# Half of a projection tile placed between the split of the first norm's sums and their products with ones

## The chip, the cores and the metric

The kernel runs on one core of one Trainium2 chip. The metric is the device time of one execution in microseconds (us). Its engines are called here as the profile calls them: PE (TensorE, matrix products), PEld (its weight loads), DVE (VectorE), ACT (ScalarE), POOL (GpSimd) and SP (SyncE, which issues nearly all DMAs). Each engine works through its own instructions in a fixed order, and waits for the others by semaphores.

## The reference

One layer (`DEPTH = 1`) on a sequence of 1024 tokens with 1024 channels, in float32. What the change touches is the very start: the first RMSNorm and the wide projection behind it.

```python
def rmsnorm(x, gain):
    xf = x.astype(jnp.float32)
    y = xf * lax.rsqrt(jnp.mean(xf * xf, axis=-1, keepdims=True) + EPS)
    return (y * gain.astype(jnp.float32)).astype(x.dtype)

def hybrid_layer(x, ...):
    h = rmsnorm(x, g_mix)
    proj = h @ w_in            # 8208 columns: attention q,k,v | forget logits | short conv |
                               # DeltaNet q,k,v, beta, decay, out gate | 3 branch gates
    ...                        # forgetting attention, gated short conv, gated DeltaNet
    x = x + merged @ w_o
    ...                        # channel mixer with a causal conv, then a per-layer embedding
    return x
```

## The kernel before

Activations lie transposed: 128 channels on the partitions, 1024 tokens along the free axis, in two halves of 512 (`NB[0]`, `NB[1]`; `nb` counts them). Eight such tiles `xg` hold the normed input's channels, without the norm's factor: `xg` is x times the gain, and the factor per token, `rs`, is multiplied in when a projection is copied out of PSUM. Since a matrix product takes operands of reduced precision (`fp32r`), each float32 operand is split into a high part (an ACT copy) and a low part (a DVE or POOL subtraction, x - high), and each product is three matmuls: high by high, high by low, low by high. A 128x128x512 block so costs three matmuls, and one output half of a projection tile (8 blocks, `KT = 8`) 24.

A **raw tile** is a projection of 128 output channels that is written to HBM as it is, without `rs`, for later use. `raw_tile(u)` loads and splits its weight (`wr`, then `wo` for the two halves of its rows) and returns a function `evac(nb, ps)` that copies a finished half from PSUM with ACT (`o<-sm` or `o<-mm`, line 504) and stores it to `raw[u]` by an SP DMA (line 505).

`first_norm()` runs in this order of code:

- It loads x tile by tile, makes `xg` (lines 270 and 271), adds up the squares over the eight tiles in `acc[0]` and `acc[1]` (lines 278 and 280), and meanwhile multiplies the few logits (`few`), the first query tile (`pq`) and one raw tile (`pr_`).
- `make_rstd(acc)` forms `rs`. For each half it splits the sums into `h` (ACT, line 289) and `l` (DVE, line 290), multiplies both with a 128x128 matrix of ones (two matmuls into one PSUM bank), and takes the inverse square root with three ACT operations (lines 257 to 259) and two DVE operations (lines 260 and 264). `between` is a hook that another norm uses: work that is put between the splits and the products. Here it is not given.
- A second raw tile is multiplied, half 0 and then half 1, each into a bank of the role `sm`.

The buffers count: `h` and `l` have one buffer each (`h=1, l=1` in the phase `fx`), the split weights `wo` five (`WO = 5`), and the role `sm` five PSUM banks in this phase, two in the next one; the roles `mm` and `ev` have two and one.

After it come, in the code, the logits (`few_logits`: the `sm` tile times `rs`, eight small transposes at line 396, and two DVE copies at lines 399 and 400), the query and key tiles, `scalars()` (a chain of some fifty small DVE operations on the logits that ends in `gall`, line 456; PE transposes `gall` at line 458, and it goes to HBM as `cdr` and comes back as `cb` for the attention), the value tile (copied out with a multiplication by `rs` at line 543, transposed by PE into the bank `ev` at line 546, copied out of it at lines 549 and 550), and the attention with projection tiles between its blocks.

The order on each engine isn't that of the code. A scheduler with a timeline of its own (`schedule_with_timeline_sim=True`) places each instruction when it is built, so a local edit can reorder a stretch behind it. Instructions that are given `tc.issue_after(x)` are placed behind x.

Of the kernel before, what the change touches and what calls it, by code (L numbers as in the profile page):

```python
# [48 lines left out]
def hybrid_block(ctx: ExitStack, tc: tile.TileContext, I, out, dbg=None):  # L49
# [5 lines left out]
    def nm(s):  # L55
        uid[0] += 1
        return f"{s}_{uid[0]}"
# [25 lines left out]
    def pt(tag, bufs, w=512, dt=F32):  # L83
        pool, n = homes.setdefault(tag, (scopes[-1], bufs))
        return pool.tile([P, w], dt, tag=tag, name=nm(tag), bufs=n)

    def bank(role):
        pool, n = homes[role]
        return pool.tile([P, 512], F32, tag=role, name=nm(role), bufs=n)
# [4 lines left out]
    def smb():  # L94
        return bank("sm")
# [4 lines left out]
    def tmp(role="tmp", dt=F32, w=512):  # L100
        return pt(role if role in homes else "tmp", 0, 516, dt)[:, 0:w]
# [21 lines left out]
    pe = [None]  # L123

    def mm(o, l, r, start, stop, more=False):
        pe[0] = nc.tensor.matmul(o, lhsT=l, rhs=r, start=start, stop=stop, skip_group_check=more)  # L126
# [20 lines left out]
    def wload(src, n=1024, eng=None):  # L147
        wr = wraw(src, n)
        return [wsplit(wr[:, c : min(c + 512, n)], eng or weng[0]) for c in range(0, n, 512)]

    def step(ps, w, j, x, nb, first, last):
        h, l = x
        wh, wl = w[j // 4]
        sl = slice(j % 4 * P, j % 4 * P + P)
        mm(ps, wh[:, sl], h[:, NB[nb]], first, False)
        mm(ps, wh[:, sl], l[:, NB[nb]], False, False)
        mm(ps, wl[:, sl], h[:, NB[nb]], False, last)
# [93 lines left out]
    def rsqrt(ps, scale, neg=False, t=None):  # L251

        w = ps.shape[-1]
        y = tmp("y") if w == 512 else small(w)
        if t is None:
            t = tmp("t") if w == 512 else small(w)
        S.activation(t, ps, AF.Ln, scale=scale)
        S.activation(y, t, AF.Exp, scale=-0.5)
        S.activation(t, y, AF.Square)
        V.scalar_tensor_tensor(out=t, in0=t, scalar=(0.5 if neg else -0.5) * scale, in1=ps, op0=ALU.mult, op1=ALU.mult)  # L260
        return t, y

    def newton(o, t, y, neg=False):
        V.scalar_tensor_tensor(out=o, in0=t, scalar=-1.5 if neg else 1.5, in1=y, op0=ALU.add, op1=ALU.mult)

    def norm_operand(kt, x, c):

        h, l = (xp.tile([P, T], F32R, tag="xg", name=nm("xg")) for _ in range(2))
        for nb in range(2):
            S.activation(h[:, NB[nb]], x[:, NB[nb]], AF.Copy, scale=col(c + kt))  # L270
            V.scalar_tensor_tensor(out=l[:, NB[nb]], in0=x[:, NB[nb]], scalar=col(c + kt),
                                   in1=h.bitcast(F32)[:, NB[nb]], op0=ALU.mult, op1=ALU.subtract)
        return h, l

    def sumsq(acc, x, first, eng=(G, G)):
        for nb in range(2):
            sq = acc[nb] if first else tmp("sq")
            last = S.activation(sq, x[:, NB[nb]], AF.Square).ins  # L278
            if not first:
                eng[nb].tensor_tensor(out=acc[nb], in0=acc[nb], in1=sq, op=ALU.add)  # L280
        return last

    def make_rstd(acc, between=None):

        r = cp.tile([P, T], F32, tag="rs", name=nm("rs"))
        parts = []
        for nb in range(2):
            h, l = tmp("h", F32R), tmp("l", F32R)
            S.activation(h, acc[nb], AF.Copy)
            V.scalar_tensor_tensor(out=l, in0=acc[nb], scalar=D * EPS / P, in1=h.bitcast(F32),  # L290
                                   op0=ALU.add, op1=ALU.subtract)
            parts.append((h, l))
        after = between() if between else None
        for nb in range(2):
            h, l = parts[nb]
            ps = smb()
            with tc.issue_after(after) if after else nullcontext():
                mm(ps, ones_r, h, True, False)
                mm(ps, ones_r, l, False, True)
            newton(r[:, NB[nb]], *rsqrt(ps, 1.0 / D))  # L300
        return r
# [22 lines left out]
    def first_norm():  # L324
        ones_f = pt("ones_f", 1, P)
        V.memset(ones_f, 1.0)
        V.tensor_copy(ones_r, ones_f)
        wsr, wsp = pt("wsr", 1, P), pt("wsp", 1, 256, F32R)
        pair = wsp.rearrange("p (k t c) -> p k t c", t=2, c=16)
        S.dma_start(wsr, I["wsm"])  # L330
        S.activation(pair[:, :, 0], wsr.rearrange("p (k c) -> p k c", c=16), AF.Copy)
        V.tensor_tensor(out=pair[:, :, 1], in0=wsr.rearrange("p (k c) -> p k c", c=16),
                        in1=pair[:, :, 0].bitcast(F32), op=ALU.subtract)
        acc = [pt("acc", 2) for _ in range(2)]
        xr = [pt("xr", 8, T) for _ in range(KT)]
        few, pq, pr_ = ([bank(r) for _ in range(2)] for r in ("sm", "mm", "sm"))
        for kt in range(KT):
            for nb in NB if kt == 0 else (slice(0, T),):
                Q.dma_start(xr[kt][:, nb], I["xT"][kt][:, nb])
            xg.append(norm_operand(kt, xr[kt], C_G1))  # L340
            if kt == 0:
                wq = wload(I["win"][U_FQ], eng=V)
            if kt == 2:
                wr, _, _, evac = raw_tile(spare["r"].pop(0), V)
            if kt:
                sumsq(acc, xr[kt - 1], kt == 1, (V, V))
        sumsq(acc, xr[KT - 1], False, (V, V))
        for kt in range(KT):
            for nb in range(2):
                h, l = xg[kt]  # L350
                for n, x in ((32, h), (16, l)) if kt == 0 else ((16, l), (32, h)):
                    mm(few[nb][:n], wsp[:, kt * 32 : kt * 32 + n], x[:, NB[nb]], kt == 0 and n == 32,
                       kt == KT - 1 and n == 32)
            for w, ps in ((wq, pq), (wr, pr_)):
                for nb in range(2):
                    step(ps[nb], w, kt, xg[kt], nb, kt == 0, kt == KT - 1)
        for nb in range(2):
            evac(nb, pr_[nb])
        Q.dma_start(cst, I["cst"])
        Q.dma_start(rows, I["rows"])  # L360
        V.tensor_copy(bd_r, bdf)
        V.tensor_copy(U_r, Uf)
        early[U_FQ] = pq
        rs = make_rstd(acc)
        w, _, _, evac = raw_tile(spare["r"].pop(0))
        for nb in range(2):
            ps = bank("sm")
            for kt in range(KT):
                step(ps, w, kt, xg[kt], nb, kt == 0, kt == KT - 1)
            evac(nb, ps)  # L370
        return rs, few

    def exp32(x):
# [124 lines left out]
    def raw_tile(u, eng=None):  # L498

        raw[u] = dr.tile([P, T], F32, tag=f"r{u}", name=f"r{u}")  # L500

        def f(nb, ps):
            o = tmp("o")
            S.activation(o, ps, AF.Copy)  # L504
            Q.dma_start(raw[u][:, NB[nb]], o)
        return wload(I["win"][u], eng=eng), KT, xg, f
# [383 lines left out]
    with phase("fx", psum=dict(mm=MM, ev=1), cv=3, o=4, sg=2, h=1, l=1, y=1,  # L890
               smt=1, Y=1, ye=1, en=1, er=1, Yz=1, Yq=1, lfh=1, lfl=1):
        with phase("f0", psum=dict(sm=5), tmp=8):
            rs, few = first_norm()
            smt = few_logits(few)
# [64 lines left out]
    with phase("la", psum=dict(mm=6, sm=2), a=16, wq=3):  # L959
        with phase("me", tmp=9, sg=4, yr=4):  # L960
# [83 lines left out]
            acc = [tmp() for _ in range(2)]  # L1044
# [120 lines left out]
        with phase("do", tmp=8, sg=4):  # L1165
# [23 lines left out]
            acc = [tmp() for _ in range(2)]  # L1189
# [96 lines left out]
```

## Time and profile before

| what | us |
|---|---|
| three runs | 1966.53, 1966.87, 1961.18; median 1966.53 |
| the profiled execution | 1961.41, of which 1959.6 is the profile's span |
| PE busy | 1927.2 of the span (98%) |
| DVE busy | 1337.7 (68%) |
| ACT busy | 914.6 (47%) |
| POOL busy | 530.6 (27%) |
| granted PE clock, mean | 0.999 of full speed |

How to read it: times in the views below are counted from the start of the span. A row of the timeline has the start, the duration, engine, line, operation, what it writes and reads, and how many like it follow each other (`x24`, then the duration is from the first's start to the last's end). A bracket says how long the engine was idle ahead of it and whose end released it. The PE is busy nearly throughout, so time can come or go only where it waits, and it waits seldom.

### The profile page before, as it was taken

To read this page: it belongs to the slowest core of one execution; us is meant where nothing else is said; L and a number is where in the kernel's file an instruction comes from. 1 tells how busy PE (TensorE), PEld (TensorE's weight loads), DVE (VectorE), ACT (ScalarE), POOL (GpSimd) and SP (SyncE) were. 2 spreads that over 40 slices of the span, in tenths; PEclk is the share of its full clock that TensorE was granted. 3 is DMA by queue.
4 is the path that set the end of the run, shared out by engine and by line. 5 is a ranking of instruction groups with operands and counts; after the bars stand their busy time and mean duration, and the time that the engine had idled before them with its cause. 6 is when DMAs were issued, how large, how long until landed. Compare 5 with 4: busy or idle time off the path is not lost.

```text
span 1959.6 us, 25470 instructions
## 1 busy us (share of the span) xinstructions
PE 1927.2 (98%) x9281; PEld 1602.3 (82%) x9281; DVE 1337.7 (68%) x2172; ACT 914.6 (47%) x1660; POOL 530.6 (27%) x431
## 2 busy tenths in 40 slices
PE   8999999999999999999999999999999999999998
PEld 6888888888888888888788787788888888888887
DVE  6878788879488124438767538888888888444564
ACT  6576777677422233433433326555454454111351
POOL 1446343434322221100034112244333431000200
PEclk9999999999999999999999999999999999999999
DMA  4222112121442153347863523212212218322132
GB/s 180 71 89 69 59 60 73 68 69 55 136 130 102 44 170 119 105 180 261 285 220 118 188 107 111 74 57 84 97 65 97 72 55 292 97 86 87 44 119 86
DMA packets 102926, 219.42 MB, mean 112 GB/s; under 512 B 9392, under 2 KB 40720, under 8 KB 102800
## 3 DMA queue, kind: packets, MB, share of 16 engines
q1 hardware_dynamic: 102512, 217.61, 32.7%
q8 instruction: 73, 1.20, 0.3%
q14 instruction: 53, 0.43, 0.1%
q10 hardware_dynamic: 288, 0.18, 0.0%
HBM read 158.98 MB, written 58.77 MB: 111 GB/s over the span
## 4 chain that ended last, share of the span: by engine, by line
PE 78%; DVE 11%; ACT 4%; DMA 3%; issue 3%; POOL 1%; SPq 0%; DVEq 0%; ACTq 0%; POOLq 0%
PE mm L126 68%; PE sm L126 5%; DVE o L492 1%; PE py L126 1%; PE ev L126 1%; PE pq L638 1%; DMA sg<-r 1%; DVE wo L130 1%; PE po L126 1%; DMA y<-yr 1%; DVE pl L130 1%; DVE o L1099 1%; ACT pp L601 1%; DVE st L526 1%; POOL ws L199 1%
## 5 line engine op out<-in xcount | busy, mean ns | idle before, releaser
L126 PE MATMUL mm<-xg,wo 128*128 128x512 f32 x6128 | 1478.1, 392 | 7.8 <-DVE wo L130 2.2
L126 PEld LDWEIGHTS mm<-xg,wo 128*128 128x128 f32 x6128 | 1139.4, 188 | 245.2 <-DVE wo L130 3.5
L126 PE MATMUL mm<-a,wo 128*128 128x512 f32 x1216 | 303.5, 389 | 1.4 <-DVE sg L1034 1.4
L129 ACT ACTIVATE wo<-wr 128x512 fp32r<-128x512 f32 x252 | 157.2, 627 | 277.9 <-PE mm L126 268.1
L126 PEld LDWEIGHTS mm<-a,wo 128*128 128x128 f32 x1216 | 228.3, 188 | 49.4 <-DVE sg L1034 1.8
L130 POOL TENSOR_TENSOR wo<-wr,wo 128x512 fp32r<-128x512 f32 x108 | 148.8, 1381 | 327.1 <-ACT wo L129 324.4
L1186 DVE TENSOR_TENSOR a<-mm,a 128x512 f32<-128x512 f32 x96 | 65.3, 689 | 92.1 <-PE mm L126 91.9
L130 DVE TENSOR_TENSOR wo<-wr,wo 128x512 fp32r<-128x512 f32 x144 | 106.9, 744 | 26.6 <-ACT wo L129 26.1
L280 POOL TENSOR_TENSOR tmp<-tmp,tmp 128x512 f32<-128x512 f32 x21 | 28.1, 1339 | 293.3 <-ACT tmp L278 293.3
L1035 POOL TENSOR_TENSOR a<-a,sg 128x512 f32<-128x512 f32 x28 | 42.3, 1518 | 207.6 <-DVE sg L1034 207.6
L1099 DVE SCALAR_TENSOR_TENSOR o<-cw,cols,o 128x1024 f32<-128x1024 f32 x44 | 77.3, 1757 | 0.1
L492 DVE SCALAR_TENSOR_TENSOR o<-cv,cols,o 128x512 f32<-128x512 f32 x72 | 70.0, 972 | 10.2 <-ACT o L490 9.1
L504 ACT ACTIVATE o<-mm 128x512 f32<-128x512 f32 x60 | 35.7, 594 | 78.5 <-PE mm L126 47.5
L601 ACT ACTIVATE pp<-pp,small 128x512 f32<-128x512 f32 (+2 forms) x96 | 58.4, 610 | 28.7 <-DVE small L595 28.4
L1131 POOL TENSOR_TENSOR cg<-o,cg 128x1024 f32<-128x1024 f32 x22 | 54.8, 2492 | 61.0 <-ACT cg L1130 61.0
L130 DVE TENSOR_TENSOR wo<-wq,wo 128x512 fp32r<-128x512 f32 x48 | 65.5, 1367 | 5.1 <-ACT wo L129 4.2
L129 ACT ACTIVATE wo<-ws 128x512 fp32r<-128x512 f32 x80 | 50.2, 630 | 33.3 <-PE mm L126 33.2
L199 POOL TENSOR_TENSOR ws<-wq,wr 128x512 f32<-128x512 f32 x20 | 44.0, 2199 | 79.7 <-DVE wo L130 74.7
L1099 DVE SCALAR_TENSOR_TENSOR o<-cg,cols,o 128x1024 f32<-128x1024 f32 x44 | 58.5, 1329 | 5.4 <-ACT o L1097 5.2
L130 DVE TENSOR_TENSOR pl<-pq,ph 128x512 fp32r<-128x512 f32 (+1 forms) x80 | 49.9, 629 | 13.9 <-ACT ph L129 13.5
L199 POOL TENSOR_TENSOR ws<-wr 128x512 f32<-128x512 f32 x20 | 35.8, 1792 | 71.6 <-DVE ws L199 54.9
L230 ACT ACTIVATE u<-mm 128x512 f32<-128x512 f32 x20 | 12.0, 599 | 80.0 <-PE mm L126 80.0
(295 smaller groups left out, 2414.0 us busy)
## 6 DMA issues: line engine op xcount, KB each, us to landing
wr<-win SPq DMA_DIRECT2D x64, 512.0 KB, 3.6
r<-o SPq DMA_DIRECT2D x64, 256.0 KB, 2.6
wq<-wup SPq DMA_DIRECT2D x24, 512.0 KB, 3.5
wr<-wup SPq DMA_DIRECT2D x20, 512.0 KB, 3.7
ad<-o SPq DMA_DIRECT2D x20, 512.0 KB, 3.9
wq<-ad SPq DMA_DIRECT2D x20, 512.0 KB, 4.5
wr<-wdn SPq DMA_DIRECT2D x20, 512.0 KB, 3.7
yr<-r SPq DMA_DIRECT2D x16, 512.0 KB, 4.8
```

The source lines that it names most:

```text
L126: pe[0] = nc.tensor.matmul(o, lhsT=l, rhs=r, start=start, stop=stop, skip_group_check=more)
L129: S.activation(h, x, AF.Copy)
L130: (eng or V).tensor_tensor(out=l, in0=x, in1=h.bitcast(F32), op=ALU.subtract)
L199: (G if e == "g" else V).tensor_tensor(out=o, in0=x, in1=y, op=op)
L280: eng[nb].tensor_tensor(out=acc[nb], in0=acc[nb], in1=sq, op=ALU.add)
L492: V.scalar_tensor_tensor(out=o, in0=cv[:, i : i + 512], scalar=col(c0 + i), in1=o, op0=ALU.mult, op1=ALU.add)
L504: S.activation(o, ps, AF.Copy)
L601: S.activation(t[:, :w], t[:, :w], AF.Exp, bias=mn[:, k - 1 : k], scale=-1.0, accum_out=sm[:, i : i + 1])
L1035: (V if b == 2 and dt > 5 else G).tensor_tensor(out=m, in0=m, in1=t, op=ALU.add)
L1099: V.scalar_tensor_tensor(out=o, in0=cv[:, i : i + T], scalar=col(c0 + i), in1=o, op0=ALU.mult, op1=ALU.add)
L1131: G.tensor_tensor(out=sg, in0=o, in1=sg, op=ALU.mult)
L1186: V.tensor_tensor(out=x2[dt][:, NB[nb]], in0=ps, in1=x2[dt][:, NB[nb]], op=ALU.add)
```

## The change

`first_norm()` hands half 0 of the second raw tile to `make_rstd` as `between`; half 1 follows behind. `half` returns PE's last instruction, and the products with ones are placed behind it.

```diff
         early[U_FQ] = pq
-        rs = make_rstd(acc)
         w, _, _, evac = raw_tile(spare["r"].pop(0))
-        for nb in range(2):
+
+        def half(nb):
             ps = bank("sm")
             for kt in range(KT):
                 step(ps, w, kt, xg[kt], nb, kt == 0, kt == KT - 1)
             evac(nb, ps)
+            return pe[0].ins
+        rs = make_rstd(acc, lambda: half(0))
+        half(1)
         return rs, few
```

All lines behind it move by 3: line 504 of before is 507 of the changed kernel, 456 is 459. The number of instructions is the same on each engine. Their order differs from the 129th matmul row on, up to about the 800th (roughly the first 190 us); behind that it is the same on all engines.

On PE, behind the first raw tile (`sm_171`), before, the products of the sums with ones (`h` and `l` of half 0, then `h` of half 1) and the second raw tile's half 0 (`sm_466`):

```order
L126 MATMUL sm_171<-xg_272,wo_210 128x512
L126 MATMUL sm_437<-h_429,ones_r 128x512
L126 MATMUL sm_437<-l_430,ones_r 128x512
L126 MATMUL sm_447<-h_433,ones_r 128x512
L126 MATMUL sm_466<-xg_174,wo_460 128x512
```

The same place now; the first row is the last of the 24 matmuls of half 0 (`sm_446`), and `sm_494` is half 1:

```order
L126 MATMUL sm_446<-xg_272,wo_434 128x512
L126 MATMUL sm_474<-h_438,ones_r 128x512
L126 MATMUL sm_474<-l_439,ones_r 128x512
L126 MATMUL sm_484<-h_442,ones_r 128x512
L126 MATMUL sm_494<-xg_174,wo_431 128x512
```

The three products have moved behind 24 matmuls. The fourth, of `l` of half 1, moves with them from within half 0 to the 22nd place of half 1.

On ACT, before, from the split of a later weight (`wo_789`) on: the split `h` of half 1, the inverse square root of half 0 (lines 257 to 259), the first step of that of half 1, and the raw tile's copy:

```order
L129 ACTIVATE wo_789<-wr_787 128x512
L289 ACTIVATE h_433<-acc_157 128x512
L257 ACTIVATE tmp_441<-sm_437 128x512
L258 ACTIVATE y_440<-tmp_441 128x512
L259 ACTIVATE tmp_441<-y_440 128x512
L257 ACTIVATE tmp_451<-sm_447 128x512
L504 ACTIVATE o_491<-sm_466 128x512
```

The same place now:

```order
L129 ACTIVATE wo_789<-wr_787 128x512
L507 ACTIVATE o_471<-sm_446 128x512
L289 ACTIVATE h_442<-acc_157 128x512
L257 ACTIVATE tmp_478<-sm_474 128x512
L258 ACTIVATE y_477<-tmp_478 128x512
L259 ACTIVATE tmp_478<-y_477 128x512
L129 ACTIVATE wo_792<-wr_787 128x512
L257 ACTIVATE tmp_488<-sm_484 128x512
```

The copy of the raw tile's half 0 (`o_471`) stands ahead of the split `h_442` of half 1, and a weight's split ahead of the second inverse square root.

On DVE, some 45 us later, before: the end of the chain of small operations (`Yq`, then `gall`), and behind it the copy of a DeltaNet tile (`cv`, line 691), three convolution steps (line 492) and a step of a key's norm (`sg_681`, line 260), which frees the bank `ev`:

```order
L455 TENSOR_TENSOR Yq_764<-Yq_764,Yz_763 128x8
L264 SCALAR_TENSOR_TENSOR o_628<-sg_630,o_628 128x512
L456 TENSOR_TENSOR gall<-sm_758,Yq_764 128x96
L464 TENSOR_TENSOR kdx<-Yz_763,gall 128x32
L526 SCALAR_TENSOR_TENSOR st_593<-o_628,cols,st_591 64x512
L466 SCALAR_TENSOR_TENSOR nbe<-eG,beta 128x32
L691 TENSOR_TENSOR cv_896<-mm_871,rs_428 128x512
L526 SCALAR_TENSOR_TENSOR st_594<-o_628,cols,st_592 64x512
L460 COPY smt_777<-sm_775 96x128
L492 SCALAR_TENSOR_TENSOR o_899<-cv_896,cols,o_899 128x512 x3
L260 SCALAR_TENSOR_TENSOR sg_681<-sg_681,ev_687 128x512
```

Now, where `cv_896` and both steps `st_593` and `st_594` stand just ahead of these rows:

```order
L455 COPY Yz_763<-sm_757 128x96
L458 TENSOR_TENSOR Yq_764<-Yq_764,Yz_763 128x8 x4
L495 SCALAR_TENSOR_TENSOR o_899<-cv_896,cols,o_899 128x512
L458 TENSOR_TENSOR Yq_764<-Yq_764,Yz_763 128x8
L495 SCALAR_TENSOR_TENSOR o_899<-cv_896,cols,o_899 128x512
L458 TENSOR_TENSOR Yq_764<-Yq_764,Yz_763 128x8
L495 SCALAR_TENSOR_TENSOR o_899<-cv_896,cols,o_899 128x512
L458 TENSOR_TENSOR Yq_764<-Yq_764,Yz_763 128x8
L260 SCALAR_TENSOR_TENSOR sg_681<-sg_681,ev_687 128x512
L676 TENSOR_SCALAR sg_904<-o_899 128x512
L459 TENSOR_TENSOR gall<-sm_758,Yq_764 128x96
```

The convolution steps and the norm's step have moved ahead of `gall`. On PE the transposition of `gall`, which stood 36 rows earlier, inside the matmuls of `mm_926`, now stands among the transpositions of the value tile (`ev_822`), inside a raw tile (`mm_990`):

```order
L126 MATMUL mm_990<-xg_260,wo_987 128x512
L549 MATMUL ev_822<-cst,o_820 128x128 x3
L461 MATMUL sm_775<-cst,gall 96x128
L549 MATMUL ev_822<-cst,o_820 128x128
L126 MATMUL mm_990<-xg_259,wo_987 128x512
```

So `gall` now comes out on DVE behind what frees `ev`, and is asked for by PE at the same place as `ev`. On SP one weight load stands ahead of the store of `cdr` instead of behind the loads of `cb`.

## The prediction

> **What bounds the kernel now.** I read the page first, then the waits of PE, then the timeline around the change, then what depends on it on ACT and DVE. The page's first part has the busy time of each engine; the view of waits, for the first 220 us, has engine, tile and line that waited, for whom, us in total, times, longest.
>
> ```profile
> PE 1927.2 (98%) x9281; PEld 1602.3 (82%) x9281; DVE 1337.7 (68%) x2172; ACT 914.6 (47%) x1660; POOL 530.6 (27%) x431
> ...
> PE sm L126 <- DVE wsp L332: 6.8, 1, 6.8
> PE mm L126 <- ACT o L504: 1.6, 1, 1.6
> PE sm L126 <- ACT h L289: 1.3, 1, 1.3
> PE ev L126 <- DVE sg L260: 0.8, 1, 0.8
> PE ev L546 <- DVE sg L260: 0.3, 1, 0.3
> ```
>
> PE is the bound, and the number of its matmuls stays. So the time changes by PE's waits alone, and only in the stretch whose order changes, up to about 190 us. Behind the start-up (6.8 us, which the change doesn't reach) PE waits there four times, 4.0 us in sum. The change aims at the 1.3 us. What follows on PE and ACT around it:
>
> ```profile
> 37.26 1.53 PE L126 MATMUL sm<-xg,wo 128*128 128x512 f32 x6
> 38.62 0.39 PE L126 MATMUL sm<-h,ones_r 128*128 128x512 f32 x1
> 38.85 0.40 PE L126 MATMUL sm<-l,ones_r 128*128 128x512 f32 x1
> 40.51 0.50 PE L126 MATMUL sm<-h,ones_r 128*128 128x512 f32 x1 [1.26 <-ACT h L289]
> 40.84 4.97 PE L126 MATMUL sm<-xg,wo 128*128 128x512 f32 x21
> 45.65 0.39 PE L126 MATMUL sm<-l,ones_r 128*128 128x512 f32 x1
> ...
> 38.13 1.28 ACT L504 ACTIVATE o<-sm 128x512 f32<-128x512 f32 x2
> 39.31 0.62 ACT L129 ACTIVATE wo<-wr 128x512 fp32r<-128x512 f32 x1
> 39.83 0.62 ACT L289 ACTIVATE h<-acc 128x512 fp32r<-128x512 f32 x1
> 46.08 0.60 ACT L257 ACTIVATE tmp<-sm 128x512 f32<-128x512 f32 x1 [3.81 <-PE sm L126]
> ```
>
> A matmul takes 0.229 us from start to start ((45.65 - 40.84) / 21). The product of l (38.85) would be followed at 39.08; the next one starts at 40.51, so the wait costs 1.43 us, and 0.10 more since 40.51 to 40.84 is 0.33 and not 0.23. It ends with the split h of half 1 on ACT (39.83 to 40.45), which had the copies of the first raw tile and a weight's split ahead of it.
>
> **The change, step by step.** *The wait for h (-0.5).* The 24 matmuls of half 0 now start at 38.62 and end 24 x 0.229 later, at 44.12, with the last result at 44.28; the two products of half 0 follow to 44.58. The split h of half 1 can't be done ahead of all this: h has one buffer, which the product with the old h frees, now at 44.5; and on ACT the copy of half 0 stands ahead of it and waits for the last result. Behind a copy that starts at 44.32, h starts 0.5 later (39.31 to 39.83 is 0.52) and ends at 45.43; PE goes on at 45.49. It waits 0.91 and 0.10, in place of 1.43 and 0.10: a gain of 0.5. The wait moves, and what it waits for is now a copy instead of a weight's split. Bounds: all of it gone, -1.5; a wait as long as before, 0. Queued behind the copy on ACT are h and the three steps of the first half's inverse root; PE waits for h alone.
>
> *The second half of rs (nothing there, but it makes the rest late).* Its last product, l of half 1, moves from 45.65 to 45.82 + 21 x 0.229 = 50.63, so ACT's first step to 51.1 (46.08 before). Who needs it are the logits' last four transpositions, and through them the DVE chain to gall:
>
> ```profile
> 50.65 1.27 DVE L518 TENSOR_TENSOR o<-mm,rs 128x512 f32<-128x512 f32 x2
> 52.85 0.29 DVE L399 COPY smt<-sm 128x128 f32<-128x128 f32 x1 [0.93 <-PE sm L396]
> 83.64 0.25 DVE L456 TENSOR_TENSOR gall<-sm,Yq 128x96 f32<-128x96 f32 x1
> ...
> 53.00:75.00 22.00, 22.00 (x99) 18.13 (x99) 21.15 (x51) 9.45 (x18) 8.55 (x7) 1.00 0.16 57
> ```
>
> (The last row is a stretch of the windows: busy us of PE, PEld, DVE, ACT, POOL, then the granted clock, DMA's share, GB/s.) The scheduler puts a query product and 24 matmuls of the next tile ahead of those transpositions, so PE has work: from 51.85 on 26 matmuls, then four transpositions, to 58.15. The second bank of the early query, which the matmul behind them needs, is freed about 57.4 (from 51.1 three ACT steps with a copy and two splits between them, then four DVE steps of 0.7), just in time. So PE loses nothing here, but DVE's chain starts at 58.3 in place of 52.85, and DVE is busy 21.15 of 22 us in that stretch: it can't catch up.
>
> *gall (+1.8).* It took 31.04 us from the logits' copy to gall (52.85 to 83.89). The rows of what now stands ahead of gall, and of PE where it will ask for it:
>
> ```profile
> 75.81 1.66 DVE L526 SCALAR_TENSOR_TENSOR st<-o,cols,st 64x512 fp32r<-64x512 f32 x2 [0.79 <-ACT st L532]
> 85.63 0.68 DVE L691 TENSOR_TENSOR cv<-mm,rs 128x512 f32<-128x512 f32 x1
> 89.18 3.25 DVE L492 SCALAR_TENSOR_TENSOR o<-cv,cols,o 128x512 f32<-128x512 f32 x3 [1.74 <-ACT o L490]
> 92.35 0.67 DVE L260 SCALAR_TENSOR_TENSOR sg<-sg,ev 128x512 f32<-128x512 f32 x1
> 92.95 0.90 DVE L673 TENSOR_SCALAR sg<-o 128x512 f32<-128x512 f32 x1
> 102.77 0.73 DVE L492 SCALAR_TENSOR_TENSOR o<-cv,cols,o 128x512 f32<-128x512 f32 x1
> ...
> 90.23 1.65 POOL L130 TENSOR_TENSOR wo<-wr,wo 128x512 fp32r<-128x512 f32 x1 [3.63 <-ACT wo L129]
> 91.83 1.74 POOL L521 TENSOR_TENSOR o<-o,y 128x512 f32<-128x512 f32 x1
> ...
> 84.58 8.22 PE L126 MATMUL mm<-xg,wo 128*128 128x512 f32 x35
> 93.08 0.66 PE L546 MATMUL ev<-cst,o 128*128 128x128 f32 x4 [0.28 <-DVE sg L260]
> ```
>
> Moved in: two steps of a key (1.66), cv (0.68), three convolution steps (3.25), the norm's step (0.67) and a clamp (0.90), 7.16 us. Moved out, ahead of the logits' copy: a low part and a copy of a query, about 0.68 each. And 0.79 us of idle time is filled. So 58.3 + 31.0 + 7.2 - 1.4 - 0.8 = 94.3 for gall. PE came to this place at 92.61 (84.58 + 35 x 0.229) and waited until 93.08, 0.47. It will come 0.5 earlier, at 92.1, wait for sg (two rows ahead of gall on DVE) and then for gall until 94.36: 2.26, less the 0.47 that was there, +1.8. Part of it may fall earlier, at the bank of the value tile's second half. Bounds: DVE catches up, -0.5 (that wait gone); the 5.4 us of the chain's late start are paid whole, +5.4. I take the sum of rows.
>
> DVE's steps are longer beside POOL: the three convolution steps took 3.25 beside two POOL operations, and one alone 0.73. Had they stood still through the whole of both POOL rows, they would have taken 3 x 0.73 + 1.65 + 1.74 = 5.6, which is 2.3 more (rival b). I keep the row's 3.25, since the same two POOL operations stand beside the same three steps now. [...]
>
> *The raw tile's copy (-0.7).* PE's largest wait follows behind it:
>
> ```profile
> 100.07 0.62 PE L126 MATMUL sm<-st,st 128*128 128x128 f32 x4
> 102.29 0.73 PE L126 MATMUL mm<-xg,wo 128*128 128x512 f32 x2 [1.60 <-ACT o L504]
> 101.65 0.59 ACT L504 ACTIVATE o<-mm 128x512 f32<-128x512 f32 x1
> 94.38 1.18 DVE L264 SCALAR_TENSOR_TENSOR o<-sg,o 128x512 f32<-128x512 f32 x1
> ```
>
> PE needs the bank that this ACT copy frees. The copy follows, by much the same ACT operations, the DVE step that ended at 95.56; behind a gall at 94.3 (cv 0.6, the step 1.2) that is 96.1, so the copy comes at about 102.2 and PE goes on at 102.9, 0.6 later than before. PE's lag by then was -0.5 + 1.8 = +1.3, of which this wait absorbs 0.7. Bounds: the wait gone, -1.6; nothing absorbed, 0.
>
> *The rest (+0.5).* Up to 190 us the order is new. Before, PE stood still for nothing there; in a like stretch behind it, it did:
>
> ```profile
> 140.00:180.00 40.00, 40.00 (x205) 33.92 (x204) 37.42 (x70) 29.03 (x57) 24.00 (x21) 1.00 0.18 63
> 180.00:220.00 40.00, 39.22 (x201) 32.93 (x200) 31.36 (x69) 30.41 (x60) 17.97 (x14) 1.00 0.20 70
> 75.00:110.00 35.00, 33.12 (x151) 26.46 (x149) 25.85 (x46) 25.17 (x47) 18.43 (x15) 1.00 0.27 92
> ```
>
> 0, 0.78 in 40 and 1.88 in 35. For 80 us these make 0 to 4.3; the 0.8 us wait at 189 could also go. I take +0.5, nearest to the first. The SP queue: the store of cdr, the loads of cb and all behind them come some 10 us later; I cost it at nothing, because the first scores' DVE step must wait for them only near where it stood. If that cover is gone, it shows as a PE wait for pp, within these 4.3.
>
> **Sum.** -0.5 + 1.8 - 0.7 + 0.5 = +1.1 us: 1961.41 + 1.1 = 1962.5 for an execution like the profiled one (1959.6 of span, 1.8 around it). The median shown is 5.1 above that: of four executions two lie near 1961.3 and two near 1966.7, and the trace doesn't say why. Their mean is 1964.0, 2.6 above the profiled one; I add it and predict 1965.1.
>
> **Rivals.** (a) *The waits go.* h comes early enough and DVE catches up: -1.5, -0.5, -1.6 and -0.8 at the most, 1957.0 (1959.6 with the 2.6). For it: all these are short. Against it: ACT's order and the one buffer of h; DVE's 96% in 53 to 75. (b) *DVE's lag grows.* At gall: if the moved steps stand still through the whole of the POOL rows, gall comes 2.3 later, and the time is 1964.8, 1967.4 with the 2.6. This mechanism makes the kernel slower by over 0.3% (5.9 us, about what a measurement of it can tell from no change) only when gall comes 4.8 us later than I say, behind 99.1: then 1970. Against that: five more microseconds are three POOL operations of 1.65 met in full. (c) *Only the wait moves*: no DVE lag reaches PE, 1961.41 - 0.5, 1963.5 with the 2.6.
>
> **How the numbers follow.** My sum, between (c) and (b): 0.5. (c): 0.17. (a): 0.15. (b): 0.18, of which half beyond 99.1. No bound of gains reaches 5.9 us (4.4 at most); but executions lie up to 5.7 apart, so that a median can fall at either level, and faster by over 0.3% gets 0.11 from (a) and (c). Slower gets 0.09 from (b) and 0.02 from the levels: 0.11. Within 0.3%: 0.78. The range takes the lower level less half of (a)'s gain, 1959.3, to the upper level with the +3.4 that (b) gives and a little of the rest, 1971.
>
> **What would show it.** In the profile after: the copy of the raw tile (line 507) ending about 44.9 and h at 45.4, with PE waiting 0.9 for it; the logits' copy on DVE at 58.3; gall at 94.3, and PE waiting there or at the value tile's bank for 2 us; the wait for line 507 near 102.9. Wrong would be: h's wait gone (then -1.5), gall before 92 (no lag), or a PE wait of over 3 us between 60 and 190.

## The result and the profile after

The changed kernel took 1972.86 us in the median of 5 runs (1969.31 to 1975.78), the kernel before 1965.03 in its 5: ratio 1.0043, 95% interval [1.003, 1.0057]. A second series gave 1971.1 against 1964.66, ratio 1.0027 [1.0016, 1.0037]. So the change costs 6 to 8 us, where no change was forecast. The profiled execution took 1972.86 us, with a span of 1971.1.

The waits of PE from 30 to 220 us, after (engine, tile and line that waited, for whom, us in total, times, longest):

```profile
PE mm L126 <- DVE o L546: 3.0, 1, 3.0
PE ev L126 <- DVE sg L260: 1.1, 2, 0.6
PE sm L126 <- ACT h L289: 0.7, 1, 0.7
PE mm L126 <- DVE o L521: 0.7, 1, 0.7
PE ev L549 <- DVE sg L260: 0.5, 1, 0.5
PE mm L126 <- ACT o L507: 0.4, 1, 0.4
PE ev L549 <- DVE st L553: 0.3, 1, 0.3
```

The wait for h fell from 1.3 to 0.7 and that for the raw tile's copy from 1.6 to 0.4. Two larger waits are new: 0.7 for a key's multiplication (line 521), and 3.0 for the value tile's second copy (line 546), which frees the bank that the next tile's second half needs. The timeline after, rows of PE, then ACT, then DVE (start, us, engine, operation, count, idle time ahead and who ended it):

```profile
43.33 0.40 PE L126 MATMUL sm<-l,ones_r 128*128 128x512 f32 x1
44.46 0.50 PE L126 MATMUL sm<-h,ones_r 128*128 128x512 f32 x1 [0.74 <-ACT h L289]
50.62 0.43 PE L399 MATMUL sm<-cst,sm 32*128 32x32 f32 x4
57.12 0.43 PE L399 MATMUL sm<-cst,sm 32*128 32x32 f32 x4
84.46 2.06 PE L126 MATMUL mm<-xg,wo 128*128 128x512 f32 x5 [2.96 <-DVE o L546]
106.70 5.51 PE L126 MATMUL mm<-xg,wo 128*128 128x512 f32 x23 [0.36 <-ACT o L507]
...
43.30 0.60 ACT L507 ACTIVATE o<-sm 128x512 f32<-128x512 f32 x1 [4.33 <-PE sm L126]
43.79 0.62 ACT L289 ACTIVATE h<-acc 128x512 fp32r<-128x512 f32 x1
...
57.58 0.29 DVE L402 COPY smt<-sm 128x128 f32<-128x128 f32 x1
83.78 0.63 DVE L546 TENSOR_TENSOR o<-mm,rs 128x512 f32<-128x512 f32 x1
97.93 0.24 DVE L459 TENSOR_TENSOR gall<-sm,Yq 128x96 f32<-128x96 f32 x1
```

The logits' eight transpositions are now four at 50.62 and four at 57.12; their copy on DVE comes at 57.58 (52.85 before), the value tile's second copy ends at 84.41, and gall comes at 97.93 (83.64 before). The next matmul in PE's queue needs that bank, and PE stood for 2.96 us. Before, the row of the same copy was this:

```profile
80.37 0.68 DVE L543 TENSOR_TENSOR o<-mm,rs 128x512 f32<-128x512 f32 x1
```

It ended at 81.05, and PE started the first matmul that needs its bank at 82.02. So the copy had only 0.97 us to spare, and the chain that it stands in now starts 4.73 us later (52.85 to 57.58). Behind the wait, PE of the changed kernel went on slowly: five matmuls in 2.06 us, where four starts 0.229 apart and one matmul of 0.4 make 1.3. Two stretches of the windows after show why (busy us of PE, PEld, DVE, ACT, POOL with counts, then the granted clock, DMA's share, GB/s):

```profile
81.60:85.00 3.40, 0.54 (x2) 0.48 (x3) 3.26 (x12) 0.03 (x1) 0.39 (x1) 1.00 0.00 0
85.01:88.42 3.41, 3.41 (x12) 2.81 (x10) 2.62 (x5) 2.25 (x4) 0.00 (x0) 0.50 0.00 0
```

Behind a stretch in which PE was busy for 0.54 of 3.40 us, its clock was granted at 0.50 for 3.41 us. DVE is busy for 3.26 us while PE waits: it has work, and PE waits for its turn in that work.

The loads of the start end up to 0.8 us apart from one execution to the next, so I count from PE's matmul number 128, the first that the change touches (the product with h at 38.62 before, the first of half 0 at 37.65 after):

```
PE's matmul number        182    280    330    366    420    700    829   1400
before, us from 128     13.66  35.20  45.96  54.63  67.74 123.09 150.71 259.84
after, us from 128      13.12  35.95  51.72  60.36  72.81 128.23 155.80 265.78
lag                     -0.54  +0.75  +5.76  +5.73  +5.07  +5.14  +5.09  +5.94
```

Nearly all of the loss arises between the matmuls 280 and 330: the 3 us wait and the half clock behind it. (The same number isn't quite the same work: gall's short transposition stands ahead of 330 before and behind it now, which makes some 0.3 of the lag there.) From 900 on the order of PE is the same in both kernels.

### The profile page after: what moved, and what is told of

Its sections match the earlier page's. It is cut to its first block, busy times and chain, and to the rows that moved or that the text cites. A ratio compares the mean times of both kernels' runs of the same rounds, so it can differ in the third digit from the quotient of the medians.

```text
span 1971.1 us, 25469 instructions
## 1 busy us (share of the span) xinstructions
PE 1933.5 (98%) x9281; PEld 1605.5 (81%) x9281; DVE 1339.7 (68%) x2172; ACT 913.7 (46%) x1660; POOL 531.7 (27%) x431
## 4 chain that ended last, share of the span: by engine, by line
PE 77%; DVE 11%; DMA 5%; ACT 4%; issue 3%; POOL 1%; SPq 0%; DVEq 0%; ACTq 0%; POOLq 0%
PE mm L126 66%; PE sm L126 6%; DVE o L495 1%; PE py L126 1%; PE ev L126 1%; PE pq L641 1%; DMA kc<-kdr 1%; DVE wo L130 1%; DMA sg<-r 1%; DMA y<-yr 1%; DVE o L1102 1%; PE po L126 1%; DMA yr<-r 1%; DVE st L529 1%; DVE l L476 1%
## 5 line engine op out<-in xcount | busy, mean ns | idle before, releaser
L126 PE MATMUL sm<-st,st 128*128 128x512 f32 (+2 forms) x192 | 49.8, 351 | 0.0
```

## Experiments

Four questions: do these rows come back; is the cause the late second half of rs or the place of the logits' transpositions in the queue; does POOL hold up DVE; does the half clock come from idle time.

**The kernel before, again.** No edit.

> The kernel before, unchanged, to see what its own executions differ by. Theory 'windows': the two levels of its times (1961 and 1967 us) are stretches of halved TensorE clock behind long PE waits for the transfer kc<-kdr (about 545 us); then slower executions show a mean clock of .998 instead of .999, and each window of 3.4 us at half clock costs about 1.7 us. Rival 'transfers': slower executions have the same mean clock, and the time goes into longer waits for transfers alone. A median of 1963 to 1966 us either way.

1966.17 us, ratio to the other runs of before 1.0002 [0.9992, 1.0011]. At the wait for the raw tile's copy, 1.60 us at 102.29 in the first profile and again 1.60 us here, the two executions part (timeline, and windows of this execution):

```profile
101.48 0.73 PE L126 MATMUL mm<-xg,wo 128*128 128x512 f32 x2 [1.60 <-ACT o L504]
```

```profile
99.00:102.40 3.40, 1.80 (x11) 1.21 (x10) 1.91 (x3) 3.35 (x7) 1.81 (x2) 1.00 0.04 13
102.42:105.83 3.41, 3.41 (x12) 2.73 (x10) 3.38 (x7) 0.33 (x2) 1.30 (x1) 0.50 0.43 126
```

Here the wait was followed by half clock, in the first profile it was not. Both executions stand at 54.6 us at matmul 366, and at 67.74 and 69.36 at matmul 420: the window costs 1.62 us. This execution has four of them ahead of its end (at 102, 546, 850 and 1263 us), the first profile has none. Over 83 executions of the kernel before, the time goes with the mean granted clock:

```
mean clock            1.000    0.999    0.998    0.997    0.996    0.995
executions                1       24       31       19        6        2
mean time, us       1961.43  1963.48  1965.13  1966.76  1968.12  1969.40
```

So the levels of before, for which the prediction had no reason, are in large part the number of half-clock windows. "Windows" holds, though they stand at four places and not only at the transfer that it named.

**The changed kernel, again.** No edit.

> The changed kernel, unchanged. Theory 'order': its wait of 3.0 us for the value tile's copy (line 546, 84 us) and the half-clock window there come from the order of the instructions, so they come back within 0.5 us; the waits for kc<-kdr at 552 us and the half-clock windows at 552 and 856 us come from transfers and may be missing. Rival 'chance': the wait at 84 us was one execution's, and this profile has it under 1.5 us with no half-clock window before 110 us. 1970 to 1974 us by the first, 1966 or less by the second.

1971.1 us. The wait for line 546 came back at 3.0 us, with half clock from 86.6 to 90.0 us, and the lag at matmul 829 is the same to 0.01 us. "Order" holds. The windows at 551 and 855 us came back too, but those stand at the like places in most profiles of either kernel.

**Two buffers for h and l, changed kernel.**

```diff
-            h, l = tmp("h", F32R), tmp("l", F32R)
+            h, l = (pt(n + "2", 2, 512, F32R) if between and "h" in homes else tmp(n, F32R) for n in "hl")
```

> The changed kernel with two buffers each for h and l in the first norm, so that both sums are split before half 0 and all four products with ones stand right behind it; the order of PE from row 181 on and of the DVE chain stays nearly that of the changed kernel. Theory 'place of the logits' transpositions' (the second four stand behind a query product and 24 matmuls of the next tile): the 0.74 us wait for h goes, the logits' copy stays at 57 to 58 us, the 3 us wait for line 546 and the half clock there stay: 1969 to 1972 us. Rival 'late product' (the second half of rs is late because its product with l stands behind 21 matmuls): the copy comes by 54 us, the wait at 84 us falls under 1 us, no half clock there: 1962 to 1965 us.

1971.02 us, ratio to before 1.0023 [1.0013, 1.0032]. The timeline, PE and DVE, and a row of PE's waits:

```profile
44.14 0.40 PE L126 MATMUL sm<-h,ones_r 128*128 128x512 f32 x1
44.37 0.40 PE L126 MATMUL sm<-l,ones_r 128*128 128x512 f32 x1
56.81 0.43 PE L399 MATMUL sm<-cst,sm 32*128 32x32 f32 x4
...
51.71 0.68 DVE L396 TENSOR_TENSOR sm<-sm,rs 32x512 f32<-32x512 f32 x1
57.28 0.29 DVE L402 COPY smt<-sm 128x128 f32<-128x128 f32 x1 [2.90 <-PE sm L399]
```

```profile
PE mm L126 <- DVE o L546: 3.3, 1, 3.3
```

The products of the second half follow at once and h's wait is gone. DVE has used the second half of rs by 52.39 (51.71 + 0.68), and later stands idle for 2.90 us until PE comes to the second four transpositions, at 56.81. The stall at line 546 stays, at 3.3 us, and with it comes half clock from 82.73 to 89.56 us. So "late product" falls: what counts is that these transpositions are queued on PE behind a query product and nearly the whole first half of the key tile.

**The same, with the transpositions ahead.** The query's and key's work on PE is queued behind the eighth transposition:

```diff
-            nc.tensor.transpose(pst[:, t * 32 : t * 32 + 32], sm32[:32, t * P : t * P + P], ident[:32, :32])
+            pe[0] = nc.tensor.transpose(pst[:, t * 32 : t * 32 + 32], sm32[:32, t * P : t * P + P], ident[:32, :32])
...
-            for k in "qk":
-                proj[0][0](k)
+            with tc.issue_after(pe[0].ins):
+                for k in "qk":
+                    proj[0][0](k)
```

> As the changed kernel with two buffers for h and l, and the query's and key's matmuls queued behind all eight transpositions of the logits. Theory 'place of the transpositions' (and with it the DVE chain behind the logits' copy): the copy at 51 to 53 us, no wait over 1 us for line 546, no half-clock window before 110 us; PE may stand up to 1 us at the transpositions: 1961 to 1966 us. Rival 'DVE is full anyway': DVE's work up to 85 us is the same, so a wait of 2 to 3 us for line 546, 543 or the like stays between 80 and 100 us, and the time is 1968 to 1973 us.

The timeline of DVE:

```profile
53.87 0.28 DVE L402 COPY smt<-sm 128x128 f32<-128x128 f32 x1
84.11 0.26 DVE L459 TENSOR_TENSOR gall<-sm,Yq 128x96 f32<-128x96 f32 x1
```

No wait for line 546 and no half clock ahead of 273 us; gall is back at 84.11, and at matmul 420 this kernel is 0.45 us ahead of before. (PE stood 1.8 us at the transpositions, which was more than expected.) But the time is 1976.09 us, ratio 1.0047 [1.0035, 1.006], far over the 1961 to 1966 expected: its order differs further on, in the attention, and from matmul 420 to 1400 it loses 8.5 us against before. There PE waits 5.8 us for DVE (before 1.5) and 1.1 us for an ACT copy, and one half-clock window is added. Why that order is worse was not settled; the run speaks for the first 110 us alone.

**The transpositions late, the half not moved.** The kernel before, with the second four transpositions and the logits' copy written behind the first 24 matmuls of the key tile (where `hook` is run):

```diff
-            smt = few_logits(few)
+            sm32 = few_logits(few)
...
+            turn_logits(sm32, pst, range(4))
+            proj[0][0]("q")
...
+            def rest():
+                with tc.issue_after(pe[0].ins):
+                    turn_logits(sm32, pst, range(4, 8))
+                smt.append(sum_logits(pst))
+            hook.append(rest)
+            proj[0][0]("k")
```

> The kernel before (half 0 not moved), only with the second four transpositions of the logits queued behind the query product and the first 24 matmuls of the next tile, where the changed kernel has them. Theory 'place of the transpositions': logits' copy at 57 to 58.5 us, a PE wait of 2 to 4 us for the value tile's second copy at 82 to 86 us with a half-clock window behind it, gall behind 93 us: 1969 to 1972 us, though the half was not moved. Rival 'the half itself' (ACT's or DVE's steps of the first norm displace the chain): wait for the value tile's copy under 1 us, 1964 to 1966 us.

1970.88 us, ratio 1.0028 [1.0018, 1.0038]: as slow as the changed kernel in its second series. The timeline, PE and DVE:

```profile
84.72 1.42 PE L126 MATMUL mm<-xg,wo 128*128 128x512 f32 x5 [2.15 <-DVE o L551]
97.16 0.66 PE L554 MATMUL ev<-cst,o 128*128 128x128 f32 x4 [1.87 <-DVE sg L264]
...
60.12 0.28 DVE L407 COPY smt<-sm 128x128 f32<-128x128 f32 x1
100.27 0.26 DVE L464 TENSOR_TENSOR gall<-sm,Yq 128x96 f32<-128x96 f32 x1
```

At matmul 420 it stands at 72.53 (changed 72.81, before 67.74). Two details miss the expectation: the logits' copy comes at 60.12, and the half clock comes not behind the wait of 2.15 us for the value tile (line 551 here) but behind the next one, of 1.87 us, at 97.9 us. The cause is shown from both sides: the transpositions ahead take the stall away, the transpositions late make it, with the half where it was.

**The start's weights on DVE.** The changed kernel, with the six low parts of the start's three tiles made by DVE instead of POOL:

```diff
+            weng[0] = V
             filler(PLAN["start"])
+            weng[0] = G
```

> The changed kernel with the low parts of the weights of the three tiles of the start (six steps) made by DVE instead of POOL; DVE has then six steps of about 0.65 us more, POOL six fewer of 1.3 to 1.8 us. Theory 'short DVE steps stand still beside POOL' (steps of 0.25 us that took 1.3 us when a POOL step ran): the chain to the value tile's second copy gets no longer in spite of the added steps, the copy ends by 84 us and the wait for it is under 2.5 us: 1966 to 1970 us. Rival 'DVE is full': the added steps are paid in whole, the copy ends at 86 us or later, wait 4 us or more: 1973 to 1976 us.

1967.21 us, ratio to before 1.0008 [0.9998, 1.0017], 4 us under the changed kernel. The timeline of the changed kernel, DVE and POOL:

```profile
77.43 1.35 DVE L435 SCALAR_TENSOR_TENSOR en<-en,Yq 128x96 f32<-128x96 f32 x1
79.59 3.38 DVE L435 SCALAR_TENSOR_TENSOR en<-en,Yq 128x96 f32<-128x96 f32 x5
...
77.38 1.29 POOL L130 TENSOR_TENSOR wo<-wr,wo 128x512 fp32r<-128x512 f32 x1 [1.12 <-ACT wo L129]
78.90 1.82 POOL L130 TENSOR_TENSOR wo<-wr,wo 128x512 fp32r<-128x512 f32 x1 [0.24 <-ACT wo L129]
80.69 1.29 POOL L524 TENSOR_TENSOR o<-o,y 128x512 f32<-128x512 f32 x1
```

And of this one, DVE:

```profile
75.80 0.69 DVE L130 TENSOR_TENSOR wo<-wr,wo 128x512 fp32r<-128x512 f32 x1
77.74 0.55 DVE L435 SCALAR_TENSOR_TENSOR en<-en,Yq 128x96 f32<-128x96 f32 x2
78.98 0.68 DVE L546 TENSOR_TENSOR o<-mm,rs 128x512 f32<-128x512 f32 x1
```

A step of 96 columns takes 0.27 us by itself (two in 0.55). Beside the POOL step that began 0.05 us earlier and ran for 1.29, it took 1.35; five beside the next two POOL steps took 3.38, 2.0 more than by themselves. On DVE a low part takes 0.69. From the logits' copy to the end of the value tile's second copy it is 21.7 us now (57.96 to 79.66), and was 26.8 (57.58 to 84.41), though DVE does more work. Some 1.5 of these 5.1 us are order: four of the short steps and two others now stand behind the copy. The wait for line 546 is gone and so is the half clock behind it. "DVE is full" falls. New waits behind 110 us (1.6 us for a low part of the attention, 0.8 for a minimum) keep this kernel above before.

**PE busy instead of waiting.** The changed kernel with 11 more matmuls ahead of the first half of the tile that follows the value tile:

```diff
+            for i in range(fill.pop() if fill else 0):
+                mm(ps, w[0][0][:, 0:P], mov[0][0][:, NB[0]], True, True)
             for j in range(kts):
...
+            fill.append(11)
             filler(PLAN["start"])
```

> The changed kernel with 11 extra matmuls (2.5 us, their result thrown away) ahead of the key tile behind the value tile, so that PE reaches the wait for the value tile's second copy 2.5 us later; the copy's own time is unchanged. Theory 'half clock from the idle time': wait 0.3 to 0.8 us, no half-clock window at 82 to 92 us, so that the extra matmuls cost nothing and 1.4 to 1.7 us are gained: 1968.5 to 1970.5 us. Rival 'half clock for another reason' (load, or a fixed time): the window stays, 1971 to 1973 us.

A miss: 1973.71 us, ratio 1.0043 [1.0029, 1.0057]. The order put a product of the scalars ahead of the second half's matmuls, and PE waited there instead:

```profile
86.67 0.31 PE L126 MATMUL sm<-lfh,ones_r 128*128 128x96 f32 x1 [2.67 <-ACT lfh L129]
```

The half clock followed, at 88.0 us. The wait was moved and hardly made shorter, so the run can't tell the two theories apart by time. What speaks for idle time is that the half clock came behind waits for four different things (DVE's copy, 2.96 us; ACT's split, 2.67; ACT's copy, 1.60; a transfer, 2.91 at 552.0 in the changed kernel). The pair of executions of before, one with half clock behind the same 1.60 us and one without, leaves it open.

**Two buffers in the kernel before.** The edit of the two buffers alone, with the half where it was.

> The kernel before (half 0 not moved) with two buffers each for h and l in the first norm: both sums are split at once and the four products with ones stand together; the order of PE behind them stays. Theory 'the wait is the gain': the 1.3 us wait for h and its 0.1 behind it go, nothing takes their place, the logits' copy comes 1.5 us earlier: 1.0 to 1.5 us under before (1963 to 1964 us where before has 1964.7). Rival 'absorbed': the next waits (sg at 93 us, the raw tile's copy at 102 us) grow by as much, 0 to 0.5 us gained.

1964.35 us against 1965.69, ratio 0.9992 [0.9983, 1.0000]; at matmul 420 it is 1.56 us ahead of before. The interval reaches 1, so the time alone doesn't show a gain; the trace does, for the lead is still 1.57 us at matmul 1400. "The wait is the gain" holds: what the change went after is worth about 1.5 us, and a second buffer takes it without moving a tile.

**Both edits, on either kernel.**

> The kernel before with two buffers for h and l, and the low parts of the start's six weight halves on DVE instead of POOL. Theory 'POOL steps hold up DVE': with six POOL steps fewer the raw tile's copy and the sg steps come no later; the waits of 1.6, 0.8 and 0.3 us up to 110 us shrink in sum: 0 to 2 us under the two-buffer kernel (1964.35), 1962.5 to 1964.4. Rival 'DVE is full': DVE, 96% busy from 53 to 75 us, takes 4 us more of work and the value tile's copy or sg is waited for: 1965 to 1969 us.

> The changed kernel with both edits: two buffers for h and l, and the start's low parts of weights on DVE. Its logits' second transpositions stay late (after the query product and 24 matmuls). Theory: the 0.74 us wait for h goes as in the two-buffer form of the changed kernel, and no wait for the value tile's copy comes, as with the weights on DVE alone (1967.2): 1965.5 to 1967 us, still over the kernel before with two buffers (1964.35), since the late gall and the waits behind 110 us stay. Rival 'the half between helps once nothing is late': 1964 us or less.

The kernel before with both took 1961.16 us, ratio to before 0.9978 [0.9969, 0.9986]: faster than both kernels, and than I had expected. PE's waits from 30 to 220 us are down to two:

```profile
PE mm L126 <- ACT o L504: 1.2, 1, 1.2
PE ev L126 <- DVE sg L260: 0.3, 1, 0.3
```

At matmul 829 it is 3.4 us ahead of before (147.30 against 150.71). The changed kernel with both took 1964.35 us, ratio 0.9998 [0.9987, 1.001], under the range that I gave and 3.2 us above the former: with the stall gone, half 0 between still earns nothing.

## Why the prediction was wrong

By its own steps, with lags from matmul 128:

- *The wait for h (-0.5)*: right. -0.54 at matmul 182, with the raw tile's copy at 43.30 and h at 43.79 on ACT ahead of the product at 44.46.
- *The second half of rs (nothing)*: the logits' copy at 57.58 was as forecast (58.3, where matmul 128 came at 38.62 and not at 37.65). But 1.3 us were lost up to matmul 280, 0.7 of them in a wait for the key's multiplication, and of the two reasons given, the late product and the queue, only the second bears: with the product early the copy stayed at 57.28. The place of the transpositions in PE's queue sets it.
- *gall (+1.8)*: the step that failed. DVE's late chain met PE at the bank of the value tile's second copy, 13 us ahead of gall. The step named this bank in half a sentence, as a place where part of the wait might fall, and gave it no price, though only 0.97 us were to spare there. It measured +5.0 between the matmuls 280 and 330: 3.0 of wait, some 1.6 of half clock, and 0.3 by the count. At gall's place PE waited 0.48 (0.28 before). The step also kept DVE's durations of before. From the logits' copy to gall, the 64 DVE steps that both kernels have there took 33.8 us where they had taken 30.5, since other short steps now met POOL steps: five took 3.38 where 2.43 stood, and those of lines 382 to 384 took 1.30, 0.96 and 1.30 where 0.21, 0.21 and 0.20 stood. That is the larger part of why gall came at 97.93 and not at 94.3. Rival (b) priced this at the three convolution steps; these took 3.35 in sum, close to the row that was kept. That a step can stand still through a whole POOL row was seen at the shorter steps instead: that of line 384 took 1.30, from 64.65 to 65.95, beside a POOL step from 64.57 to 65.88.
- *The raw tile's copy (-0.7)*: right, -0.66 from matmul 366 to 420.
- *The rest (+0.5)*: 0.0 from matmul 420 to 829. Passing the SP queue cost nothing.
- *The clock* was in no step: each wait was priced at its length. The sign that was named, a PE wait of over 3 us between 60 and 190, came within 0.04 us.
- *The base (+2.6)*: near; the mean of 83 executions of before is 1965.3 where 1964.0 was taken.

At matmul 829 the sum is +5.1 instead of +1.1. To the end the changed kernel loses some 1.5 us more (1971.9 in the mean of 13 executions, against 1965.3). The two first profiles lie 11.5 us apart because that of the changed kernel has two more half-clock windows and longer waits for a transfer at about 550 us; whether the change bears on these places stays open.

## What to carry to other kernels

When a move makes a chain late on an engine that is nearly full, walk that engine's queue from there on and price the first bank or buffer that it frees for the bounding engine, not the end of the chain. A PE wait of two or three microseconds can cost more than its length: here 1.6 us more where half clock followed. A wait that comes from one buffer with two users is first a case for a second buffer, and only then for a new order.

## What the runs showed of the hardware

The granted clock fell to 0.50 for 3.41 us behind waits shorter than that: 2.96 us (at 85.0), 1.87 (97.9), and 1.60 in one execution but not in another (102.4). A wait of 2.15 us (at 84.7, with the transpositions late) was not followed by it. In the changed kernel's first profile half clock began at 85.01, 552.63 and 856.42 us: 467.62 and 303.79 apart, which is 137 and 89 times 3.413. Counted in such stretches, each one in which PE stood for more than 0.55 of the time was followed by half clock in the twelve profiles (in this one 0.84 of the stretch ahead of 85.01 and 0.82 of that ahead of 552.63); between 0.46 and 0.55 some were (0.47, ahead of 102.42, in the second profile of before) and some were not (0.51, from 1266.0 to 1269.4, in this one). Below 0.46 two cases were: the place at 850 us named at the end (0.33, ahead of 856.42), and one in the run with two buffers for h and l in the changed kernel, where half clock lasted for two stretches, 6.83 us, and PE stood for 0.36 of the first of them. So half clock also came behind a stretch in which PE was busy for about half of the time (1.80 of 3.40 us, that second profile). Why equal waits differ was not shown. At about 850 us even a wait of 1.12 us, among products of 2 columns, was followed by half clock in ten of the twelve profiles; no run tried why.
